# The RWKV-7 scan of a two-layer trunk: one product per head for scores and token-major keys, and loads in ten parts

## The chip, the cores and the metric

The kernel runs on one core of a Trainium2 chip. The metric is the device time of one execution in microseconds. The core has TensorE (PE in the rows; its loads of weights are listed apart as PEld), VectorE (DVE), ScalarE (ACT), GpSimd (POOL) and SyncE (SP). Each engine works through its own instructions in order and waits on semaphores for the others. Transfers are issued by SP, POOL and ACT and share 16 DMA engines.

## The reference

The trunk has two layers over 1024 latent and 256 context tokens of 1024 channels. The first mixes by pooling and attention, the second by a bidirectional RWKV-7 recurrence with 16 heads of 64 channels; each is followed by an MLP. The change touches the recurrence alone:

```python
def wkv_scan(s0, decay, k, v, kk, a, r, reverse):
    ...
    def step(S, inp):
        w_t, k_t, v_t, kk_t, kka_t = inp[:5]
        S = (S * w_t[:, :, None, :]
             - jnp.einsum('bhij,bhj->bhi', S, kk_t)[..., None] * kka_t[:, :, None, :]
             + v_t[..., None] * k_t[:, :, None, :])
        y = jnp.einsum('bhij,bhj->bhi', S, inp[5]) if emit else None
        return S, y
...
    for d, reverse in enumerate((False, True)):
        decay_c, k_dc, a_c = dirs_c[d]
        s_ctx, y_c = wkv_scan(s0, decay_c, k_dc, v_c, kk_c, a_c, r_c, reverse)
        decay, k_d, a = dirs[d]
        _, y_d = wkv_scan(s_ctx, decay, k_d, v, kk, a, r, reverse)
```

Both directions start on the context tokens, whose outputs aren't needed in this layer, and go on over the latent ones.

## The kernel before

The recurrence is computed in chunks of 64 tokens. Per chunk, direction and head it becomes products of 64x64 tiles: scores between tokens of the chunk, the inverse of a triangular matrix made from them, and products with the state that is carried from chunk to chunk. A stage ahead of the scan writes, per chunk and direction, four features per head to DRAM (`ft`). The scan loads them as FT, a tile of 128 partitions with eight pairs of heads: the even head of a pair lies on partitions 0 to 63, the odd one on 64 to 127 (`e` in the code), and the four features of 64 tokens stand behind each other. Features 2 and 3 of a head are the keys and their like, which serve as the 128 weight columns of a product; features 0 and 1 are the read side and the removal side.

The scan (`l1_scan`, from about 2213 to 2677 us) has 20 steps: 4 of context, then 16 of latent tokens. A step has two halves, one for each direction `d`. Each half works on the chain of chunk `s` (`chain_x`, `carry`, `chain_u`, `readout_state`, `chain_s`, `readout_values`) and, in between, on what chunk `n = s + 1` needs beforehand (`scores_k`, `token_major`, `stack`, `scores_r`; with `d` = 1 also `compose1` and `compose2`, which put together the inverse from blocks of 32). All of it is issued in the order in which it stands in the loop, under a manual schedule, so the order of each engine is that of the code. `fill()` puts a paced number of operations of a background generator between them: inverses of blocks on VectorE (L1511, L1515) up to about step 13, then parts of the readout.

Names on TensorE in a half step, in order: `xp` (chain_x, L1669), `sa` (scores_k, L1602), `tm` (token_major, four transposes of 128x128 for heads 0 to 3, L1632), `up` (chain_u, L1677), with `d` = 1 the first `p` (compose1, L1644), `tm` again, `yp` (readout_state, L1688), `sp` (chain_s, L1716), `yp` (readout_values, L1700), `sr` (scores_r, L1618), with `d` = 1 the second `p` (compose2, L1658). Context halves have no `yp` and no `sr`. A float32 matmul of the code stands as two instructions in the profile.

ScalarE copies results out of PSUM: `XS` from `xp`, `D<-up`, `TM` from `tm`, `yt` from `yp`, `p1s` and `TT` from `p`, and inside SBUF `D<-SS` (carry) and `Z<-FT` (stack). VectorE multiplies the scores by masks: `Z<-sa` (L1604), `Q<-sr` (L1622), and updates the state SS (L1722 and L1726). `sa`, `sr` and `tm` share a pool of four PSUM tiles of one bank each. GpSimd issues the load of FT, 1 MB, two steps ahead at the end of each half; SyncE issues the loads of the inverses' blocks (G, ZT, TT; eight transfers) at the end of a step, the values (`D<-v1scr`) and the stores of `yt`.

Of the kernel before, what the change touches and what calls it, by code (L numbers as in the profile page):

```python
# [58 lines left out]
class Trunk:  # L59
# [1466 lines left out]
    def l1_scan(self):  # L1526
        nc, a = self.nc, self.a
        with ExitStack() as es:
# [5 lines left out]
            scps = self.pool(es, "scps1", 4, PSUM)  # L1534
# [3 lines left out]
            FTs = [cp.tile([128, 8, 4, CH], F32, name=f"FT{i}") for i in range(4)]  # L1538
# [4 lines left out]
            st = (slice(0, 64), slice(64, 128))  # L1543

# [9 lines left out]
            W = {s: dict(lat=s >= NCC, F=[0, 0], Z=[0, 0], Q=[0, 0], TM=[0, 0], D=[0, 0], Y=[0, 0]) for s in range(NSTEP)}  # L1554
# [20 lines left out]
            def load_inverses(s):  # L1575
                w = W[s]
                TT = TTs[s % 2]
                ZT = zs.tile([128, 2, 8, 32], F32, tag="ZT", name="ZT")
                G = zs.tile([128, 2, 8, 32], F32, tag="G", name="G")
                q = lambda x, bl, e: x.rearrange("(s b c e) i t -> i s b e c t", s=2, b=2, e=2)[:, s % 2, bl, e]  # L1580
                dq = nc.sync
                for e in range(2):
# [6 lines left out]
                w["TT"], w["ZT"], w["G"] = TT, ZT, G  # L1589

            def stack(s, d):

                for e in range(2):
                    nc.scalar.copy(out=W[s]["Z"][d][0:64, :, e], in_=W[s]["F"][d][st[e], :, 1])

            def scores_k(s, d):
                F = W[s]["F"][d]
                Z = W[s]["Z"][d] = zp.tile([128, 8, 2, CH], F32, tag="Z", name="Z")
                sa = scps.tile([128, 8, CH], F32, tag="sc", name="sa")
                for h in range(8):  # L1600
                    for e in range(2):
                        nc.tensor.matmul(out=sa[st[e], h], lhsT=F[st[e], h, 3], rhs=F[st[e], h, 1], start=True, stop=True)  # L1602
                for e in range(2):
                    nc.vector.tensor_tensor(  # L1604
                        out=Z[64:128, :, e], in0=sa[st[e]], in1=masks[st[e], d, 2:3].to_broadcast([64, 8, CH]), op=ALU.mult
                    )

            def scores_r(s, d):

                w = W[s]  # L1610
                if not w["lat"]:
                    return
                F = w["F"][d]
                Q = w["Q"][d] = zp.tile([128, 8, 2, CH], F32, tag="Q", name="Q")
                sr = [scps.tile([128, 8, CH], F32, tag="sc", name="sr") for _ in range(2)]
                for h in range(8):
# [4 lines left out]
                for e in range(2):  # L1621
                    nc.vector.tensor_tensor(  # L1622
                        out=Q[:, :, e], in0=sr[e], in1=masks[:, d, 1:2].to_broadcast([128, 8, CH]), op=ALU.mult
                    )

            def token_major(s, d, h0):
                w = W[s]
                if h0 == 0:
                    w["TM"][d] = zp.tile([128, 8, 128], F32, tag="TM", name="TM")
                tm = scps.tile([128, 4, 128], F32, tag="sc", name="tm")  # L1630
                for j in range(4):
                    nc.tensor.transpose(  # L1632
                        out=tm[:, j], in_=w["F"][d][:, h0 + j, 2:4].rearrange("p a t -> p (a t)"), identity=self.ident
                    )
                nc.scalar.copy(out=w["TM"][d][:, h0:h0 + 4], in_=tm)

            def compose1(s):

                w = W[s]
                p1 = chps.tile([128, 2, 8, 32], F32, tag="ch", name="p1")  # L1640
# [6 lines left out]
                w["p1"] = zs.tile([128, 2, 8, 32], F32, tag="p1s", name="p1s", bufs=1)  # L1647
# [16 lines left out]
            def chain_x(s, d):  # L1664
                w = W[s]
                xp = chps.tile([128, 8, CH], F32, tag="ch", name="xp")
                for h in range(8):
                    for e in range(2):
                        nc.tensor.matmul(out=xp[st[e], h], lhsT=w["Z"][d][:, h, e], rhs=w["D"][d][:, h, e], start=True, stop=True)  # L1669
# [11 lines left out]
            def readout_state(s, d):  # L1681
# [4 lines left out]
                for h in range(8):  # L1686
                    for e in range(2):
                        nc.tensor.matmul(  # L1688
                            out=yp[st[e], h], lhsT=w["F"][d][st[e], h, 0], rhs=SS[d][st[e], h], start=h == 0, stop=True,
# [3 lines left out]
            def readout_values(s, d):  # L1693
# [4 lines left out]
                for h in range(8):  # L1698
                    for e in range(2):
                        nc.tensor.matmul(  # L1700
                            out=yp[st[e], h], lhsT=w["Q"][d][:, h, e], rhs=w["D"][d][:, h, e], start=False, stop=True, skip_group_check=True
# [7 lines left out]
            def chain_s(s, d):  # L1709
# [9 lines left out]
                t = hp_.tile([128, 8, CH], F32, tag="t", name="t", bufs=1)  # L1719
                src = sp  # L1720
                if s:
                    nc.vector.tensor_tensor(out=t, in0=sp, in1=SS[d], op=ALU.add)  # L1722
                    src = t
# [57 lines left out]
            for d in range(2):  # L1781
                scores_k(0, d)
                stack(0, d)
                for h0 in (0, 4):
                    token_major(0, d, h0)
# [9 lines left out]
            for s in range(NSTEP - 1):  # L1795
# [4 lines left out]
                for d in range(2):  # L1800
# [81 lines left out]
    def readout_weight(self, k):  # L1882

        if k not in self.rst:
            self.readout_weight_load(k)
        ip, zp = self.rwp
        pool, tag = {
            8: (ip, "M"), 0: (ip, "X"), 1: (zp, "TM"), 2: (ip, "BK"), 3: (zp, "Z"), 4: (zp, "Q"), 5: (zp, "TM"), 6: (zp, "Z"), 7: (zp, "Q"),
        }[k]
        w = [pool.tile([128, D], F32R, tag=tag, name=f"rwo{i}{k}") for i in "hl"]  # L1890
# [327 lines left out]
```

## Time and profile before

| | us |
|---|---|
| median of 3 runs | 3549.33 |
| range of the 3 runs | 3537.39 to 3551.44 |
| the profiled execution | 3559.48 |
| its span in the profile | 3557.6 |

The profile and its trace are of one execution, and its rows add up to its own span, which is 10 us longer than the median. Its mean granted clock of TensorE is 0.962 of full speed. Times in rows are microseconds from the start of the span, durations are microseconds unless a row says ns, and idle time of an engine that nobody waits for costs nothing.

### The profile page before, as it was taken

What the parts mean: (1) busy time and instruction counts of PE and PEld (TensorE: products, weight loads), DVE (VectorE), ACT (ScalarE), POOL (GpSimd) and SP (SyncE); (2) the same over time, 40 slices, a digit from 0 to 9 for tenths busy, and PEclk for the clock granted to TensorE, in tenths of its full rate; (3) what the DMA queues carried; (4) which work ended last, traced back from release to release, by engine and by line L of the source; (5) the groups of instructions that cost most, each with busy time, mean ns of one, the idle gap of its engine ahead of it and who ended that gap; (6) DMA issues with size and microseconds to landing.
All of it is one profiled execution on the core that took longest, in us unless ns stands there. A gap on an engine that the chain in (4) does not pass through costs nothing. (4 is left out here: it accounts for less than half of the span.)

```text
span 3557.6 us, 64666 instructions
## 1 busy us (share of the span) xinstructions
PE 3327.8 (94%) x26794; PEld 2790.3 (78%) x26794; DVE 2054.7 (58%) x3879; ACT 1432.3 (40%) x2667; POOL 342.3 (10%) x450
## 2 busy tenths in 40 slices
PE   8999889999999999989988876899988899999998
PEld 4787767888888888868878776788886788888887
DVE  4255555344444444596658996888775734444446
ACT  4244446312121211266767664655554521111112
POOL 0010110000000000024420001010031200000000
PEclk9999989999999999999989897899988999999999
DMA  8433344222222211143227678777773411111112
GB/s 274 151 92 87 97 131 130 89 83 83 83 84 83 74 46 36 42 148 99 71 69 221 210 233 241 170 185 201 200 204 104 164 50 48 48 48 48 48 48 77
DMA packets 426517, 409.24 MB, mean 115 GB/s; under 512 B 149664, under 2 KB 360480, under 8 KB 422128
## 3 DMA queue, kind: packets, MB, share of 16 engines
q1 hardware_dynamic: 405376, 321.55, 30.8%
q0 software_dynamic: 18624, 81.80, 6.8%
q8 instruction: 210, 3.44, 0.4%
q10 hardware_dynamic: 2224, 1.77, 0.2%
q14 instruction: 83, 0.68, 0.1%
HBM read 292.54 MB, written 112.49 MB: 114 GB/s over the span
## 5 line engine op out<-in xcount | busy, mean ns | idle before, releaser
L916 DVE TENSOR_TENSOR yacc<-yps,yacc 128x512 f32<-128x512 f32 x540 | 369.7, 690 | 305.2 <-PE yps L93 304.8
L74 ACT CAST wh<-st 128x1024 fp32r<-128x1024 f32 x160 | 165.0, 1049 | 759.8 <-PE yps L93 557.8
L93 PE MATMUL yps<-wh,xh 128*128 128x512 f32 x1152 | 453.8, 394 | 5.0 <-DVE yacc L916 3.4
L93 PE MATMUL yps<-wh,xl 128*128 128x512 f32 x1152 | 449.0, 390 | 0.7 <-DVE xl L75 0.7
L93 PE MATMUL yps<-wl,xh 128*128 128x512 f32 x1152 | 449.4, 390 | 0.0
L75 DVE TENSOR_TENSOR wl<-st,wh 128x1024 fp32r<-128x1024 f32 x160 | 194.2, 1228 | 277.4 <-ACT wh L74 277.2
L93 PE MATMUL acc<-h2h,wh 128*128 128x426 f32 (+3 forms) x768 | 275.1, 358 | 3.0 <-ACT y L671 3.0
L93 PEld LDWEIGHTS yps<-wh,xh 128*128 128x128 f32 x1152 | 216.4, 188 | 73.0 <-DVE yacc L916 14.0
L93 PE MATMUL acc<-h2h,wl 128*128 128x426 f32 (+3 forms) x768 | 273.6, 356 | 0.0
L93 PE MATMUL acc<-h2l,wh 128*128 128x426 f32 (+3 forms) x768 | 273.4, 356 | 0.0
L93 PEld LDWEIGHTS yps<-wh,xl 128*128 128x128 f32 x1152 | 216.5, 188 | 47.9 <-DVE xl L75 2.3
L93 PEld LDWEIGHTS yps<-wl,xh 128*128 128x128 f32 x1152 | 216.7, 188 | 44.9 <-issue 1.7
L898 DVE TENSOR_TENSOR r<-r 128x428 f32<-128x428 f32 (+4 forms) x164 | 102.4, 624 | 241.9 <-ACT r L897 241.9
L93 PE MATMUL acc<-mh,wh 128*128 128x256 f32 (+1 forms) x640 | 214.8, 337 | 4.3 <-ACT mh L74 4.2
L93 PE MATMUL acc<-ml,wh 128*128 128x256 f32 (+1 forms) x640 | 214.0, 334 | 0.0
L93 PE MATMUL acc<-mh,wl 128*128 128x256 f32 (+1 forms) x640 | 213.4, 334 | 0.0
L93 PE MATMUL acc<-h2bh,wh 128*128 128x512 f32 (+3 forms) x544 | 211.3, 388 | 1.4 <-ACT wh L74 0.7
L93 PE MATMUL acc<-h2bl,wh 128*128 128x512 f32 (+3 forms) x544 | 211.1, 388 | 1.0 <-DVE h2bl L288 1.0
L93 PE MATMUL acc<-h2bh,wl 128*128 128x512 f32 (+3 forms) x544 | 210.9, 388 | 0.3 <-DVE wl L75 0.3
L897 ACT ACTIVATE r<-acc 128x428 f32<-128x428 f32 (+4 forms) x164 | 89.1, 543 | 293.0 <-PE acc L93 267.9
L93 PEld LDWEIGHTS acc<-h2h,wh 128*128 128x128 f32 x768 | 144.6, 188 | 15.9 <-issue 5.1
L74 ACT CAST xh<-r 128x428 fp32r<-128x428 f32 (+4 forms) x164 | 93.2, 569 | 148.1 <-DVE r L898 148.1
(319 smaller groups left out, 7042.1 us busy)
## 6 DMA issues: line engine op xcount, KB each, us to landing
st<-in_mlp_w SPq DMA_DIRECT2D x128, 512.0 KB
ft<-F SPq DMA_DIRECT2D x64, 512.0 KB
FT<-ft POOLq DMA_DIRECT2D x32, 1024.0 KB, 7.1
adas<-in_ada_w POOLq DMA_DIRECT2D x112, 256.0 KB, 3.8
adas<-in_ada_w SPq DMA_DIRECT2D x80, 256.0 KB
x<-x SPq DMA_DIRECT2D x28, 512.0 KB
bias<-in_bias SPq DMA_DIRECT2D x64, 192.0 KB
ls<-ls SPq DMA_DIRECT2D x80, 128.0 KB
```

The costliest lines, as they stand in the source:

```text
L74: self.nc.scalar.copy(out=hi, in_=src)
L75: self.nc.vector.tensor_tensor(out=lo, in0=src, in1=hi.bitcast(F32), op=ALU.subtract)
L93: self.nc.tensor.matmul(out=ps, lhsT=lhs[x], rhs=rhs[y], start=first and i == 0, stop=last and i == 2)
L897: nc.scalar.activation(out=r, in_=ps, func=AF.Relu)
L898: nc.vector.tensor_tensor(out=r, in0=r, in1=r, op=ALU.mult)
L916: nc.vector.tensor_tensor(out=yacc[t][:, n], in0=ps, in1=yacc[t][:, n], op=ALU.add)
```

## The change

Three products become one. For two pairs of heads at a time (`g` = 0 to 3), `scores(s, d, g)` multiplies the 128 columns of features 2 and 3 with three blocks of 64 columns that stand side by side in FT: an identity, feature 0 and feature 1. The identity's block gives the transposed keys (what `tm` gave), the second `sr`, the third `sa`, together 192 columns per head and one PSUM tile of two banks per group; the pool has two of them in place of four tiles of one bank. In context halves the middle block is left out, in the last step the identity. FT gets a fifth block per pair of heads for the identity, which VectorE writes once, eight copies ahead of the scan. VectorE masks a group at a time into one tile ZQ (Z and Q before), four times a half, and ScalarE copies the transposed keys into TM, four times a half. The copies `Z<-FT` move into `carry()`. The temporary of the state's update is gone (SS is updated in place), and `p1s` lives in G.

The load of FT becomes four parts of two pairs each, and the load of the inverses two parts, one for each `e`. They are put on a list when a half ends its `readout_values`, and issued one by one at five places of a half (`loads()`).

```diff
-            scps = self.pool(es, "scps1", 4, PSUM)
+            scps = self.pool(es, "scps1", 2, PSUM)
...
-            FTs = [cp.tile([128, 8, 4, CH], F32, name=f"FT{i}") for i in range(4)]
+            FTs = [cp.tile([128, 8, 5, CH], F32, name=f"FT{i}") for i in range(4)]
...
+            for t in FTs:
+                for e in range(2):
+                    nc.vector.tensor_copy(out=t[st[e], :, 0], in_=self.ident[st[e], st[e]].unsqueeze(1).to_broadcast([64, 8, CH]))
...
-            def load(s, d):
+            def load(s, d, parts=range(4)):
...
-                (nc.scalar if s == 0 else nc.gpsimd).dma_start(out=F[:, :, f0:], in_=self.ft[s, d, :, :, f0:])
+                for i in parts:
+                    w["got"].add((d, i))
+                    hs = slice(2 * i, 2 * i + 2)
+                    (nc.scalar if s == 0 else nc.gpsimd).dma_start(out=F[:, hs, 1 + f0:], in_=self.ft[s, d, :, hs, f0:])
+
+            due = []
+
+            def loads():
+
+                if due:
+                    due.pop(0)()
...
+            def scores(s, d, g):
...
+                ps = scps.tile([128, 2, 512], F32, tag="sc", name="sc")
+                p4 = ps[:, :, 0:384].rearrange("p e (j f t) -> p j e f t", j=2, f=3)
+                f = slice(0, 3) if w["lat"] and more else slice(1, 3) if w["lat"] else slice(0, 3, 2)
+                for j in range(2):
                     for e in range(2):
                         nc.tensor.matmul(
-                            out=sr[e][:, h], lhsT=F[st[e], h, 2:4].rearrange("p a t -> p (a t)"), rhs=F[st[e], h, 0], start=True, stop=True
+                            out=p4[:, j, e, f], lhsT=F[st[e], 2 * g + j, 3:5].rearrange("p a t -> p (a t)"), rhs=F[st[e], 2 * g + j, f],
+                            start=True, stop=True,
                         )
...
+                if w["lat"]:
                     nc.vector.tensor_tensor(
...
+                        out=w["ZQ"][d][:, hs].rearrange("p j e f t -> p j e (f t)"),
+                        in0=ps[:, :, 0:384].rearrange("p e (j n) -> p j e n", j=2)[:, :, :, CH:],
+                        in1=masks[:, d, 1:3].rearrange("p f t -> p (f t)").unsqueeze(1).unsqueeze(1).to_broadcast([128, 2, 2, 2 * CH]),
+                        op=ALU.mult,
                     )
...
+                if more:
+                    nc.scalar.copy(out=w["TM"][d][:, hs].rearrange("p j (e i) -> p j e i", e=2), in_=p4[:, :, :, 0])
...
                     for e in range(2):
                         nc.scalar.copy(out=W[s]["D"][d][0:64, :, e], in_=SS[d][st[e]])
+                    stack(s, d)
...
                     chain_x(s, d)
                     carry()
-                    scores_k(n, d)
-                    if n + 1 < NSTEP:
-                        token_major(n, d, 0)
+                    for g in range(2):
+                        scores(n, d, g)
+                    loads()
                     fill()
                     chain_u(s, d)
                     if d:
                         compose1(n)
-                    if n + 1 < NSTEP:
-                        token_major(n, d, 4)
-                    stack(n, d)
+                    scores(n, d, 2)
+                    loads()
                     fill()
                     readout_state(s, d)
                     chain_s(s, d)
                     readout_values(s, d)
+                    if s + 2 < NSTEP:
+                        for i in range(4):
+                            due.append(partial(load, s + 2, d, (i,)))
+                            if d and i % 2:
+                                due.append(partial(load_inverses, s + 2, (i // 2,)))
+                    loads()
                     fill()
-                    scores_r(n, d)
+                    scores(n, d, 3)
                     if d:
                         compose2(n)
-                    if s + 2 < NSTEP:
-                        load(s + 2, d)
+                    loads()
+                    loads()
                     fill()
-                if s + 2 < NSTEP:
-                    load_inverses(s + 2)
```

How it moves instructions, first on TensorE, in a latent half step with `d` = 1. Before:

```order
L1669 MATMUL xp<-D,Z 64x64 x16
L1602 MATMUL sa<-FT_19565 64x64 x16
L1632 MATMUL tm<-ident,FT_19565 128x128 x4
L1677 MATMUL up<-XS_19567,TT_19568 64x64 x16
L1644 MATMUL p_23217<-ZT,G 32x32 x32
L1632 MATMUL tm<-ident,FT_19565 128x128 x4
L1688 MATMUL yp<-SS,FT_19563 64x64 x16
L1716 MATMUL sp<-D,TM 64x64 x16
L1700 MATMUL yp<-D,Q 64x64 x16
L1618 MATMUL sr<-FT_19565 128x64 x16
L1658 MATMUL p_23351<-TT_19569,p1s 32x32 x32
```

And with the change, where `sc` is the new product:

```order
L1681 MATMUL xp<-D,ZQ 64x64 x16
L1628 MATMUL sc<-FT_19565 128x192 x8
L1689 MATMUL up<-XS_19567,TT_19568 64x64 x16
L1656 MATMUL p_22962<-ZT,G 32x32 x32
L1628 MATMUL sc<-FT_19565 128x192 x4
L1700 MATMUL yp<-SS,FT_19563 64x64 x16
L1728 MATMUL sp<-D,TM 64x64 x16
L1712 MATMUL yp<-D,ZQ 64x64 x16
L1628 MATMUL sc<-FT_19565 128x192 x4
L1670 MATMUL p_23081<-TT_19569,G 32x32 x32
```

Four groups of 16, 4, 4 and 16 became groups of 8, 4 and 4; the rest kept its order. With `d` = 0 the two rows of `p` are missing. On ScalarE the same half step with `d` = 0 stood as follows before:

```order
L1670 COPY XS_19566<-xp 128x512 [waits PE_49]
L1736 COPY D<-SS 64x8x64 [waits DVE_49]
L1736 COPY D<-SS 64x8x64
L1635 COPY TM<-tm 128x512 [waits PE_49]
L1679 ACTIVATE D<-up 64x8x64 [waits PE_49,Activation_49]
L1679 ACTIVATE D<-up 64x8x64 [waits Activation_49]
L1635 COPY TM<-tm 128x512 [waits PE_49]
L1594 COPY Z<-FT_19562 64x8x64 [waits DMASW6_49]
L1594 COPY Z<-FT_19562 64x8x64
L1704 COPY yt<-yp 128x512 [waits DMAHW6_49,DMAHW5_49,PE_49]
```

And with the change, with the semaphores that each waits for in brackets (DVE is VectorE's, DMASW the loads of GpSimd):

```order
L1682 COPY XS_19566<-xp 128x512 [waits PE_49]
L1747 COPY D<-SS 64x8x64 x2
L1610 COPY ZQ<-FT_19565 64x8x64 [waits DMASW2_49,DMASW3_49,DMASW1_49,DMASW0_49]
L1610 COPY ZQ<-FT_19565 64x8x64
L1646 COPY TM<-sc 128x256 [waits DVE_49] x2
L1691 ACTIVATE D<-up 64x8x64 [waits PE_49,Activation_49]
L1691 ACTIVATE D<-up 64x8x64 [waits Activation_49]
L1646 COPY TM<-sc 128x256 [waits DVE_49]
L1716 COPY yt<-yp 128x512 [waits DMAHW7_49,DMAHW0_49,PE_49]
L1646 COPY TM<-sc 128x256 [waits DVE_49]
```

The copies of FT moved from behind `D<-up` to ahead of it, two copies `TM` stand ahead of it where one did, and `TM` waits for VectorE where it waited for TensorE. On SyncE the transfers of a step stood as follows before, those of the inverses together at its end:

```order
L1584 DMA G<-ls 32x16x32
L1585 DMA ZT<-ltt_23392 32x16x32
L1588 DMA TT_19568<-lt_23391 32x16x32 x2
L1584 DMA G<-ls 32x16x32
L1585 DMA ZT<-ltt_23392 32x16x32
L1588 DMA TT_19568<-lt_23391 32x16x32 x2
L1570 DMA D<-v1scr 64x1024
L1707 DMA yscr<-yt 64x512 x2
```

And with the change:

```order
L1601 DMA G<-ls 32x16x32
L1602 DMA ZT<-ltt_22454 32x16x32
L1605 DMA TT_19569<-lt_22453 32x16x32 x2
L1583 DMA D<-v1scr 64x1024
L1719 DMA yscr<-yt 64x512 x2
L1601 DMA G<-ls 32x16x32
L1602 DMA ZT<-ltt_22454 32x16x32
L1605 DMA TT_19569<-lt_22453 32x16x32 x2
```

The second half of the inverses moved behind the values and the stores of the following half step.

## Rows read from the trace of the kernel before

**Rows 1.** The page, section 1: busy us, share of the span, instructions.

```profile
PE 3327.8 (94%) x26794; PEld 2790.3 (78%) x26794; DVE 2054.7 (58%) x3879; ACT 1432.3 (40%) x2667; POOL 342.3 (10%) x450
```

**Rows 2.** Busy us by stretch of PE, PEld, DVE, ACT, POOL; clock, DMA share, GB/s.

```profile
2213.00:2288.70 75.70, 64.77 (x1666) 57.60 (x1666) 57.42 (x136) 50.43 (x86) 7.61 (x12) 0.91 0.81 174
2288.70:2538.20 249.50, 228.81 (x5926) 209.98 (x5922) 216.65 (x521) 141.57 (x240) 23.67 (x41) 0.93 0.68 183
2538.20:2667.80 129.60, 114.88 (x2947) 105.59 (x2944) 84.06 (x100) 77.31 (x129) 35.75 (x23) 0.92 0.76 218
```

**Rows 3.** Timeline of TensorE, 2477 to 2490: start, us, engine, line, operation.

```profile
2477.51 1.15 PE L1669 MATMUL xp<-D,Z 128*64 128x64 f32 x32
2478.59 1.15 PE L1602 MATMUL sa<-FT 64*64 64x64 f32 x32
2479.67 0.66 PE L1632 MATMUL tm<-ident,FT 128*128 128x128 f32 x4
2480.26 1.15 PE L1677 MATMUL up<-XS,TT 64*64 64x64 f32 x32
...
2486.14 2.00 PE L1618 MATMUL sr<-FT 64*128 64x64 f32 x32
2488.08 1.20 PE L1658 MATMUL p<-TT,p1s 32*32 32x32 f32 x64
2489.21 1.15 PE L1669 MATMUL xp<-D,Z 128*64 128x64 f32 x32
```

**Rows 4.** Waits of TensorE, 2213 to 2668: us in total, times, longest.

```profile
PE p L1644 <- issue: 10.1, 6, 4.1
...
PE sp L1716 <- ACT D L1679: 2.5, 10, 0.5
...
PE tm L1632 <- issue: 0.3, 1, 0.3
```

**Rows 5.** Busy us by stretch, 2441.3 to 2448.1, columns as rows 2.

```profile
2441.30:2448.10 6.80, 5.97 (x83) 5.29 (x84) 5.38 (x13) 2.40 (x4) 0.00 (x0) 0.50 0.65 98
```

**Rows 6.** Timeline of all engines, 2459 to 2471; the idle time before in brackets.

```profile
2460.99 0.53 POOL L1566 DMA_DIRECT2D FT<-ft  x1 [0.72 <-ACT TM L1635]
...
2469.98 0.33 PE L1602 MATMUL sa<-FT 64*64 64x64 f32 x3 [2.36 <-issue]
```

**Rows 7.** DMA queues (packets, MB, share) and issues (KB, us to landing), 2213 to 2680.

```profile
q8 instruction: 85, 1.39, 1.3%
...
FT<-ft POOLq DMA_DIRECT2D x32, 1024.0 KB, 7.1
```

**Rows 8.** Timeline of TensorE in the attention, 160 to 162.2.

```profile
160.22 0.70 PE L731 MATMUL sc<-kT,qT 64*128 64x256 f32 x4 [0.61 <-ACT kT L338]
160.76 0.81 PE L736 MATMUL sl<-kT,qT 64*128 64x384 f32 x4
161.50 0.50 PE L93 MATMUL acc<-h1h,wh 128*128 128x512 f32 x1
```

**Rows 9.** Groups by line, 2289 to 2668: count, busy us, mean ns, idle before.

```profile
L1604 DVE TENSOR_TENSOR Z<-sa,masks 64x512 f32<-64x512 f32 x60 | 41.4, 690 | 17.2 <-PE sa L1602 16.1
L1622 DVE TENSOR_TENSOR Q<-sr,masks 128x512 f32<-128x512 f32 x62 | 39.7, 682 | 9.3 <-PE sr L1618 9.2
L1594 ACT COPY Z<-FT 64x512 f32<-64x512 f32 x60 | 37.1, 618 | 0.9
L1679 ACT ACTIVATE D<-up 64x512 f32<-64x512 f32 x60 | 35.5, 591 | 15.2 <-PE up L1677 14.3
L1635 ACT COPY TM<-tm 128x512 f32<-128x512 f32 x56 | 32.5, 581 | 7.7 <-PE tm L1632 6.9
...
L1518 DVE COPY M<-X 128x1024 f32<-128x1024 f32 x7 | 7.4, 1062 | 0.2
```

**Rows 10.** The chain that ended last, 2164 to 2240: start, us, what.

```profile
2177.66 10.23 DMA ls<-ls
```

**Rows 11.** Timeline of VectorE, 2602 to 2614.

```profile
2606.46 2.77 DVE L1955 TENSOR_TENSOR y<-y,var 128x1024 f32<-128x1024 f32 x1
```

More of the change, by code (lines that the diff above doesn't have):

```diff
@@ L1552, in rows_of @@
                 return t[c * CH:(c + 1) * CH]
-            W = {s: dict(lat=s >= NCC, F=[0, 0], Z=[0, 0], Q=[0, 0], TM=[0, 0], D=[0, 0], Y=[0, 0]) for s in range(NSTEP)}
+            W = {s: dict(got=set(), lat=s >= NCC, F=[0, 0], ZQ=[0, 0], TM=[0, 0], D=[0, 0], Y=[0, 0]) for s in range(NSTEP)}
             lt_, ltt_ = self.lt_, self.ltt_
@@ L1608, in scores_r @@
-            def scores_r(s, d):
+                    nc.scalar.copy(out=W[s]["ZQ"][d][0:64, :, e, 1], in_=W[s]["F"][d][st[e], :, 2])
+            def scores(s, d, g):
                 w = W[s]
-                if not w["lat"]:
-                    return
                 F = w["F"][d]
-                Q = w["Q"][d] = zp.tile([128, 8, 2, CH], F32, tag="Q", name="Q")
-                sr = [scps.tile([128, 8, CH], F32, tag="sc", name="sr") for _ in range(2)]
-                for h in range(8):
+                more = s + 1 < NSTEP
+                if g == 0:
+                    w["ZQ"][d] = zp.tile([128, 8, 2, 2, CH], F32, tag="ZQ", name="ZQ")
+                    if more:
+                        w["TM"][d] = zp.tile([128, 8, 128], F32, tag="TM", name="TM")
+                assert (d, g) in w["got"]
+                ps = scps.tile([128, 2, 512], F32, tag="sc", name="sc")
+                p4 = ps[:, :, 0:384].rearrange("p e (j f t) -> p j e f t", j=2, f=3)
+                f = slice(0, 3) if w["lat"] and more else slice(1, 3) if w["lat"] else slice(0, 3, 2)
+                for j in range(2):
@@ L1622, in scores_r @@
+                hs = slice(2 * g, 2 * g + 2)
+                if w["lat"]:
                     nc.vector.tensor_tensor(
-                        out=Q[:, :, e], in0=sr[e], in1=masks[:, d, 1:2].to_broadcast([128, 8, CH]), op=ALU.mult
-                    )
[L1626 to L1633, printed above, removed]
-                    )
-                nc.scalar.copy(out=w["TM"][d][:, h0:h0 + 4], in_=tm)
+                        out=w["ZQ"][d][:, hs].rearrange("p j e f t -> p j e (f t)"),
+                        in0=ps[:, :, 0:384].rearrange("p e (j n) -> p j e n", j=2)[:, :, :, CH:],
+                        in1=masks[:, d, 1:3].rearrange("p f t -> p (f t)").unsqueeze(1).unsqueeze(1).to_broadcast([128, 2, 2, 2 * CH]),
+                        op=ALU.mult,
+                    )
+                else:
+                    nc.vector.tensor_tensor(
+                        out=w["ZQ"][d][64:128, hs, :, 1], in0=p4[64:128, :, :, 2],
+                        in1=masks[64:128, d, 2:3].unsqueeze(1).to_broadcast([64, 2, 2, CH]), op=ALU.mult,
+                    )
@@ L1646, in compose1 @@
                             )
-                w["p1"] = zs.tile([128, 2, 8, 32], F32, tag="p1s", name="p1s", bufs=1)
+                w["p1"] = w["G"]
                 for e in range(2):
@@ L1668, in chain_x @@
                     for e in range(2):
-                        nc.tensor.matmul(out=xp[st[e], h], lhsT=w["Z"][d][:, h, e], rhs=w["D"][d][:, h, e], start=True, stop=True)
+                        nc.tensor.matmul(out=xp[st[e], h], lhsT=w["ZQ"][d][:, h, e, 1], rhs=w["D"][d][:, h, e], start=True, stop=True)
                 nc.scalar.copy(out=XSs[d], in_=xp)
@@ L1688, in readout_state @@
                         nc.tensor.matmul(
-                            out=yp[st[e], h], lhsT=w["F"][d][st[e], h, 0], rhs=SS[d][st[e], h], start=h == 0, stop=True,
+                            out=yp[st[e], h], lhsT=w["F"][d][st[e], h, 1], rhs=SS[d][st[e], h], start=h == 0, stop=True,
                             skip_group_check=True,
@@ L1700, in readout_values @@
                         nc.tensor.matmul(
-                            out=yp[st[e], h], lhsT=w["Q"][d][:, h, e], rhs=w["D"][d][:, h, e], start=False, stop=True, skip_group_check=True
+                            out=yp[st[e], h], lhsT=w["ZQ"][d][:, h, e, 0], rhs=w["D"][d][:, h, e], start=False, stop=True, skip_group_check=True
                         )
@@ L1781, in l1_scan @@
             for d in range(2):
-                scores_k(0, d)
+                for g in range(4):
+                    scores(0, d, g)
                 stack(0, d)
-                for h0 in (0, 4):
-                    token_major(0, d, h0)
                 load(1, d)
@@ L1886, in readout_weight @@
         ip, zp = self.rwp
[L1887 to L1890, printed above, removed]
+        if k in (3, 4, 6, 7):
+            w = zp.tile([128, 2, D], F32R, tag="ZQ", name=f"rwo{k}")
+            w = [w[:, i] for i in range(2)]
+        else:
+            pool, tag = {8: (ip, "M"), 0: (ip, "X"), 1: (zp, "TM"), 2: (ip, "BK"), 5: (zp, "TM")}[k]
+            w = [pool.tile([128, D], F32R, tag=tag, name=f"rwo{i}{k}") for i in "hl"]
         self.split(w[0], w[1], self.rst.pop(k))
```

33 lines of the change are left out of this document (12 added, 21 removed).

## The prediction

> **What bounds the kernel now.** I read the page first, for the share of each engine: TensorE is busy for 94% of the span [rows 1], so the kernel as a whole follows TensorE. That is an average over stages, and the change touches one of them, the scan, so next I cut the scan by the steps' first `xp` into three stretches [rows 2]: context steps 0 to 3 (75.7 us, 18.9 a step), latent steps 4 to 13 with background inverses on VectorE (249.5 us, 24.95 a step), and latent steps 14 to 18 without them (129.6 us, 25.9 a step). The reader is to see two things there. TensorE idles in every stretch, although it has the most work, and its mean granted clock is 0.91 to 0.93, not 1. And VectorE is busy for 216.65 of 249.5 us (87%) in the second stretch, but for 84.06 of 129.6 (65%) in the third, which nevertheless has the longest steps. So the third is bound by TensorE, and the second by both, closely.
>
> How long would a step take if TensorE never waited? The timeline of a half step at full clock [rows 3] gives it by start to next start: the half with d=1 runs from 2477.51 to 2489.21, 11.70 us. The half with d=0 lacks the two groups of `p` (1.13 each, 2488.08 to 2489.21), so it is 9.44, and a step 21.14. Against 25.9 in the third stretch 4.8 us a step are lost. The waits of TensorE [rows 4] say where: ten of their rows name "issue", from 10.1 us before `p` down to 0.3 before `tm`, 34.0 us in all over 19 steps, that is 1.8 a step; the row on the longest engine wait of the chain, `sp` on ACT's `D`, has only 2.5. The rest is the clock: after such a hole the stretch 2441.3 to 2448.1 runs at a granted clock of 0.50, the lower of the two levels (1.2 of 2.4 GHz) [rows 5]. Stretch by stretch the lost clock is 0.09 x 75.7 + 0.07 x 249.5 + 0.08 x 129.6 = 34.7 us [rows 2]. Holes and clock together are some 69 us of 455.
>
> What is late in a hole? At 2467.61 TensorE stops, and `sa` resumes at 2469.98 after 2.36 us of "issue". The load of FT had been issued 6.6 us before, at 2460.99 [rows 6]; such a load is 1 MB and takes 7.1 us to land, and the instructions come over a DMA queue of their own, 85 packets of 16 KB (1.39 MB) in the scan [rows 7]. I read the hole as an instruction packet late behind the burst of loads. The trace shows that they coincide; it does not prove the cause.
>
> **The change part by part.** *Products on TensorE.* A latent half loses `sa` 1.08 us, two `tm` of 0.59 and `sr` 1.94 [rows 3], 4.20 in all. It gains eight pairs of 64x128 products with 192 columns. No such pair exists before. The nearest are attention's: four rows (a pair) take 0.54 us at 256 columns and 0.74 at 384 [rows 8], 0.2 per 128 columns; `sr`'s pair at 64 columns takes 1.94/8 = 0.24, and 0.24 + 0.2 gives 0.44 at 192, as the line through the two attention rows does. Bounds: 0.405, if time is in proportion to columns (0.54 x 192/256), and 0.54. So eight cost 3.5 (3.2 to 4.3), and a half saves 0.7 (-0.1 to 1.0). In the context half a pair has 128 columns, some 0.34, eight 2.7 against 2.26 for `sa` and `tm`: 0.4 lost, over seven such halves 3.
>
> *The new order on ACT.* In a d=0 half ACT now runs `XS` (0.58), two `D<-SS` and two `ZQ<-FT` (0.62 each), `TM0`, `TM1` (half of 0.58 each, bounds 0.29 and 0.58), then two `D<-up` (0.59) [rows 9]. With `XS` at 1.3 us after the half's start, `TM0` ends near 4.7 and `D` near 6.25. On TensorE `xp`, two groups `sc` and `up` end at 1.08 + 1.75 + 1.08 = 3.9. The third `sc` needs `TM0` gone from its PSUM buffer, so it waits 0.8 us; then `sc` 0.88 and `yp` 1.08 end at 6.7, after `D`, and `sp` does not wait. In the d=1 half `p` (1.13) stands before the third `sc` and covers the wait. A step is thus 21.14 - 1.4 + 0.8 = 20.6 (20.0 to 22.1) in place of 21.14. What is queued behind `TM` on ACT is `D<-up`, which `sp` needs, and `yt`.
>
> *VectorE.* Four evictions of 128x512 replace two of Z (0.69) and two of Q (0.68) [rows 9]: nothing. Background work and its pace are as before. So the second stretch keeps its VectorE work, 21.7 us a step. Its idle 3.3 holds the gaps between 521 instructions and waits; I take half for gaps, so the floor is 23.3 (21.7 to 24.95). When the third `sc` is late VectorE waits too, about 1.0 a step, by the same 0.8 and its half of the next. That makes 24.3.
>
> *The loads.* Same bytes, in four parts of 256 KB and two halves of the inverses, spread over a step; SP and POOL issue more instructions, but POOL was busy for 23.67 of 249.5 us [rows 2]. TensorE also fetches fewer instructions: 16 products in place of 40 in a half. I take it that 60% of the holes and of the slow clock after them go, between none and all: a guess, halfway and a little more, as the cause is only seen to coincide. The Trainium skill, Runtime: NRT & Kernel Launch, section Instruction fetch mechanics, says that crossing a block of instructions is mostly hidden; the holes of 2.36 us don't agree with that here, though no row proves them fetches. By that page the holes are something else and this term is zero, the first rival.
>
> A new wait can come with it: the second half of the inverses goes out behind the `yscr` stores of the next step, so `p` may wait. Bounds 0 and 1 us a step; in the sum I let the 0.4 that remains of the holes stand for it.
>
> *Before the scan.* Eight copies of the identity, 64x512 each, on VectorE: half a copy of 128x1024 (1.06) each [rows 9], 4.2 us, while VectorE makes the last features. Behind them the path is one of transfers, `ls` 10.23 us [rows 10], that start when these features are done, so I count half, 2 us (0 to 4.2).
>
> *Sum.* Third stretch: 25.9 to 20.6 + 0.4 x 4.8 = 22.5, so -3.4 a step, over five -17. Second: 24.95 to 24.3, over ten -6.5. First: +3 for the products, about -3 for fewer holes, 0. Before: +2. Together -21.5. The profiled execution took 3559.48, 10 us above the median of the runs shown, 3549.33; on its base the sum is 3538.0, on the median's 3527.8.
>
> **The rivals.** A, *the holes stay*. If the holes don't come from the load's burst, or the same bytes do it in parts as well, the third stretch gains 0.5 a step (2.7), the second nothing, the prelude loses 2, and the time is 3549. For it speaks that the bytes and queues are the same; against it, the 1 MB load just ahead of the hole that is read above. The Trainium skill, DMA: Bandwidth & Descriptors, section Queues, rings and completion order, says that a DMA engine takes turns between queues by packets; by that the length of a load matters little to another queue's packet, which speaks for A, too.
>
> B, *slower: VectorE holds ACT and ACT holds TensorE*. `TM` now waits for VectorE's product of the same group. Before, it waited for TensorE alone. `TM0` and `TM1` are covered while VectorE ends the second eviction within about 1.9 us of TensorE's second group; beyond that each microsecond delays `D<-up`, `sp` and the state. In the third stretch VectorE has readout operations of up to 2.77 us [rows 11], in the second it is 87% busy. With 2 us a step over 15 steps (+30), 2 for the prelude, and 12 back from the holes, the time is 3569. Against it: VectorE's evictions stand in the same place of its order as before.
>
> C, *more: holes and clock are cured*. Then the third stretch runs at 20.6 (-26.5) and the second at VectorE's 23.3 (-16.5), +2 before: 3508. For it speaks that the lost time is there to take; against it, that other transfers share the engines: the share of the DMA engines is 0.68 to 0.81 [rows 2].
>
> **How the numbers follow.** Chances: forecast 0.46, A 0.20, B 0.16, C 0.18. Half a per cent, 17.7 us, is about what a measurement of this kernel can tell from no change. Faster than 3531.6: two thirds of the forecast's cases (its own terms vary by some 10 us), and all of C: 0.48. Slower than 3567: most of B and a little of A: 0.15. The rest, 0.37, is within. The range 3503 to 3562 takes in the forecast, A, most of C and the mild half of B. The likeliest case's own range is 3518 to 3542.
>
> **What would show it.** Right: the rows of "issue" on TensorE fall from 34 to about 14 us, the clock of steps 14 to 18 rises to 0.97, these steps take 22.5 us, eight `sc` pairs take 3.5 us, and the third `sc` waits for ACT in the d=0 half. Wrong by A: the holes keep their sum. Wrong by B: `sp` or `sc` wait for ACT, and ACT's `TM` for VectorE, by over 1 us a half. The largest single doubt is the 60%.

## The result: slower by 0.94%

With the change the kernel takes 3578.98 us (median of 4 runs, 3577.45 to 3580.91), before it 3550.39 (4 runs); the ratio is 1.0094, 95% interval 1.0075 to 1.0113. The forecast was 3528, faster, with a range of 3503 to 3562.

The stretches of the scan, cut by the steps' first `xp`, show where it went, here for one execution of the kernel after, with the columns of [rows 2].

```profile
2210.20:2295.20 85.00, 68.36 (x1537) 59.20 (x1536) 64.05 (x162) 49.71 (x99) 20.73 (x29) 0.89 0.75 159
2295.20:2557.30 262.10, 218.41 (x5126) 190.59 (x5120) 206.28 (x508) 141.94 (x280) 69.99 (x101) 0.91 0.69 172
2557.30:2690.30 133.00, 107.07 (x2570) 94.44 (x2562) 76.46 (x98) 77.90 (x146) 55.06 (x49) 0.91 0.76 207
```

Against [rows 2] the context steps grew from 75.7 to 85.0 us, steps 4 to 13 from 249.5 to 262.1, steps 14 to 18 from 129.6 to 133.0. TensorE's own work shrank in the second and third: 228.81 to 218.41 and 114.88 to 107.07 us busy. So it waits more. These are its waits from 2210 to 2690 (total us, times, longest), to be read beside [rows 4]:

```profile
PE sc L1628 <- ACT TM L1646: 41.3, 34, 2.9
PE p L1656 <- DMA ZT<-ltt: 24.7, 11, 5.1
PE up L1689 <- ACT XS L1682: 7.1, 12, 0.9
PE p L1670 <- issue: 2.8, 1, 2.8
...
PE yp L1712 <- issue: 1.4, 1, 1.4
...
PE yp L1700 <- issue: 0.5, 1, 0.5
```

The rows of issue fell from 34.0 to 4.7 us, further than forecast. In their place stand 41.3 us in which the new product `sc` waits for the copies `TM`, and 24.7 us in which `p` waits for the inverses.

**The wait for TM, with d=1.** The next three fences are timelines of the kernel after around 2410 (start, duration, engine, line): TensorE, then VectorE, then ACT.

```profile
2407.07 0.92 PE L1628 MATMUL sc<-FT 64*128 64x192 f32 x8
...
2409.00 0.92 PE L1628 MATMUL sc<-FT 64*128 64x192 f32 x8
2412.50 1.64 PE L1628 MATMUL sc<-FT 64*128 64x192 f32 x8 [2.58 <-ACT TM L1646]
2414.07 1.97 PE L1689 MATMUL up<-XS,TT 64*64 64x64 f32 x32
...
2421.05 0.92 PE L1628 MATMUL sc<-FT 64*128 64x192 f32 x8
2421.90 1.20 PE L1670 MATMUL p<-TT,G 32*32 32x32 f32 x64
```

```profile
2407.50 0.68 DVE L1733 TENSOR_TENSOR SS<-sp,SS 128x512 f32<-128x512 f32 x1
2408.22 0.69 DVE L1737 TENSOR_TENSOR SS<-SS,pcs 128x512 f32<-128x512 f32 x1
...
2411.36 0.68 DVE L1634 TENSOR_TENSOR ZQ<-sc,masks 128x512 f32<-128x512 f32 x1
```

```profile
2412.08 0.37 ACT L1646 COPY TM<-sc 128x256 f32<-128x256 f32 x1 [4.31 <-DVE ZQ L1634]
```

The fourth `sc` of a half ends at about 2408. VectorE masks it at 2411.36, behind the state's update and six background operations. Only then does ACT copy TM, at 2412.08, and only that frees one of the two PSUM buffers for the second `sc` of the next half, which has waited 2.58 us. The rest of the half runs late, and from 2412.5 to 2416 at a granted clock of 0.51 (`up` 1.97 us against 1.15). The last two rows give the price of the product: 2421.05 to 2421.90 for two pairs, 0.425 a pair, where 0.44 was forecast.

**The wait for TM, with d=0.** VectorE's mask of the fourth group, then ACT, then TensorE, where a half of the kernel after begins:

```profile
2450.02 0.68 DVE L1634 TENSOR_TENSOR ZQ<-sc,masks 128x512 f32<-128x512 f32 x1
```

```profile
2450.73 0.37 ACT L1646 COPY TM<-sc 128x256 f32<-128x256 f32 x1 [2.31 <-DVE ZQ L1634]
2451.00 1.16 ACT L1674 COPY TT<-p 32x512 f32<-32x512 f32 x2
2452.19 0.58 ACT L1682 COPY XS<-xp 128x512 f32<-128x512 f32 x1
2452.80 1.26 ACT L1747 COPY D<-SS 64x512 f32<-64x512 f32 x2
2454.08 1.25 ACT L1610 COPY ZQ<-FT 64x512 f32<-64x512 f32 x2
2455.23 0.63 ACT L1646 COPY TM<-sc 128x256 f32<-128x256 f32 x2
```

```profile
2449.70 1.15 PE L1681 MATMUL xp<-D,ZQ 128*64 128x64 f32 x32
...
2452.82 1.15 PE L1689 MATMUL up<-XS,TT 64*64 64x64 f32 x32 [0.47 <-ACT XS L1682]
2455.64 0.92 PE L1628 MATMUL sc<-FT 64*128 64x192 f32 x8 [1.67 <-ACT TM L1646]
```

This is the wait of the third `sc` that was forecast at 0.8 us; it is 1.67, after 0.47 in which `up` waits for `XS`. `XS` begins 2.49 us after `xp`; the forecast had 1.3, which is what the kernel before shows, with the copies TT in the same place ahead of it:

```profile
2465.45 1.15 PE L1669 MATMUL xp<-D,Z 128*64 128x64 f32 x32
2465.57 1.16 ACT L1662 COPY TT<-p 32x512 f32<-32x512 f32 x2 [2.48 <-PE p L1658]
2466.75 0.59 ACT L1670 COPY XS<-xp 128x512 f32<-128x512 f32 x1
```

With the change TT begins 1.2 us later, behind the fourth TM, which has waited for the mask. So the late mask of the fourth group has a share in both waits for TM. Of their 41.3 us the third group has 24.7, the second 16.6.

**The wait for the inverses.** SyncE and TensorE in step 14 of the kernel after:

```profile
2564.66 4.25 SPq L1583 DMA_DIRECT2D D<-v1scr  x1
2569.01 1.18 SPq L1719 DMA_DIRECT2D yscr<-yt  x2
2570.24 1.51 SPq L1601 DMA_DIRECT2D G<-ls  x1
2571.79 0.55 SPq L1602 DMA_DIRECT2D ZT<-ltt  x1
```

```profile
2571.49 0.24 PE L1656 MATMUL p<-ZT,G 32*32 32x32 f32 x2
2576.82 1.91 PE L1656 MATMUL p<-ZT,G 32*32 32x32 f32 x62 [5.08 <-DMA ZT<-ltt]
```

The second half of the inverses is issued when `p` is already there: SyncE spent 4.25 us on the values and then waited its turn with the stores. ZT goes out at 2571.79 and `p` resumes 5.03 us later.

### The profile page after: what moved, and what is told of

It is laid out like the page before. It is cut to its first block, busy times and chain, and to the rows that moved or that the text cites. A ratio compares the mean times of both kernels' runs of the same rounds, so it can differ in the third digit from the quotient of the medians.

```text
span 3575.9 us, 62535 instructions
## 1 busy us (share of the span) xinstructions
PE 3312.1 (93%) x25466; PEld 2760.9 (77%) x25466; DVE 2049.2 (57%) x3903; ACT 1434.6 (40%) x2743; POOL 428.7 (12%) x564
## 3 DMA queue, kind: packets, MB, share of 16 engines
q1 hardware_dynamic: 405376, 321.55, 30.4%
q10 hardware_dynamic: 2320, 1.77, 0.2%
## 5 line engine op out<-in xcount | busy, mean ns | idle before, releaser
L1628 PE MATMUL sc<-FT 64*128 64x192 f32 (+1 forms) x1280 | 149.1, 362 | 47.9 <-ACT TM L1646 42.1
```

The costliest lines, as they stand in the source:

```text
L1628: nc.tensor.matmul(out=p4[:, j, e, f], lhsT=F[st[e], 2 * g + j, 3:5].rearrange("p a t -> p (a t)"), rhs=F[st[e], 2 * g + j, f], start=True ...
```

## The experiments

Twelve kernels and three single profiles followed. From the steps' first `xp` in the timeline of each kernel (s0, s4, s14, s19) the table has the lengths between, the time of the last, and the sums of TensorE's rows of issue and of the two waits from s0 to s19, in us (a dash where there is none over 2 us); each is one execution. The last column is the measured ratio to the kernel before, with its interval.

| kernel | steps 0-3 | 4-13 | 14-18 | s19 at | issue | sc for TM | p for ZT | ratio |
|---|---|---|---|---|---|---|---|---|
| before | 75.9 | 249.5 | 129.6 | 2667.8 | 34.0 | - | 2.7 | 1 |
| before, second profile | 75.2 | 241.8 | 121.3 | 2649.3 | 30.4 | - | - | - |
| the change | 85.1 | 262.1 | 132.9 | 2690.3 | 4.7 | 41.3 | 24.7 | 1.0094 (1.0075-1.0113) |
| parts alone | 81.0 | 268.8 | 129.3 | 2681.7 | 22.1 | - | 31.2 | 1.0066 (1.0047-1.0084) |
| product alone | 88.7 | 247.4 | 130.4 | 2679.9 | 14.0 | 42.4 | 2.5 | 1.0044 (1.0029-1.0059) |
| FT in parts alone | 84.2 | 241.3 | 130.7 | 2664.2 | 36.6 | - | 3.6 | 1.0002 (0.9988-1.0016) |
| inverses first, products of before | 77.3 | 262.0 | 135.1 | 2680.1 | 26.0 | - | 2.9 | 1.0082 (1.0058-1.0106) |
| the change, fourth group ahead | 83.4 | 263.1 | 134.6 | 2689.6 | 3.7 | 23.0 | 46.1 | 1.0092 (1.0077-1.0107) |
| the change, inverses first | 83.8 | 244.9 | 128.4 | 2669.5 | 13.6 | 44.8 | 4.9 | 1.0026 (1.0015-1.0037) |
| and copies later | 79.6 | 236.5 | 133.7 | 2658.6 | 10.8 | 26.6 | 10.4 | 1.0009 (0.9997-1.0020) |
| and TM ahead of the mask | 83.1 | 241.6 | 132.0 | 2664.8 | 18.1 | - | 8.3 | 1.0022 (1.0009-1.0036) |
| copies later, inverses at the step's end | 81.2 | 237.0 | 132.7 | 2654.9 | 20.5 | 22.9 | 5.7 | 0.9986 (0.9974-0.9997) |
| the same, FT whole | 83.1 | 237.1 | 126.8 | 2656.0 | 21.2 | 25.9 | 2.4 | 0.9998 (0.9983-1.0014) |
| the same as the last but one, product split | 82.9 | 258.0 | 129.8 | 2682.5 | 18.9 | 13.9 | 3.2 | 1.0071 (1.0051-1.0091) |
| the same, not split, fourth group ahead | 80.8 | 225.9 | 127.2 | 2641.4 | 14.1 | 24.0 | 6.8 | 0.9970 (0.9958-0.9982) |

The two profiles of before differ by 8 us in each of the latent stretches, so a difference of that size between two rows says nothing; the ratios decide.

**One part of the change at a time.** The parts of the loads under the products of before (the edit is that of `load`, `load_inverses` and `loads` in the diff, nothing else):

> The kernel before, with only the loads changed: FT in four parts and the inverses in two, issued one by one at the same places as in the change; products, PSUM pool and copies as before. Theory: the holes of TensorE came from the burst of the 1 MB load, so the parts alone cure them: rows of issue on TensorE fall from 34 us to under 8, while the late second half of the inverses makes p wait 20 to 25 us as in the changed kernel. Net 0 to -20 us against before: 3530 to 3550. Rival 1, the holes went because TensorE has fewer instructions: then they stay at 25 to 34 us and with p's waits the time is 3570 or more. Rival 2, the ten parts cost time by themselves and are the whole loss: 3575 or more, with few holes.

3571.3 us, 24 more than before, and 22.1 us of issue. Two of its waits:

```profile
PE p L1655 <- DMA ZT<-ltt: 31.2, 11, 6.5
PE sa L1613 <- DMA FT<-ft: 6.1, 4, 2.6
```

The wait of `p` was longer than the 20 to 25 us expected, and the cure of the holes did not come: at most a third went. The time is the first rival's (3570 or more), with issue a little under its 25. The other part alone keeps the new products and takes the loads of before:

> The changed kernel with the loads of before (1 MB at a half's end, all inverses at a step's end). Theory: sc waits for the copies TM about as in the changed kernel (some 40 us), p's waits for the inverses fall under 5 us, and most of the holes come back (15 to 30 us of issue): 3570 to 3600, that is, the product alone is slower than before. Rival 1 (fewer instructions cure the holes): issue stays under 8 us, and with p's waits gone the time is 3545 to 3560. Rival 2 (the parts are the whole loss): 3530 to 3550, faster than before.

3565.7 us, 18 more than before: the product alone is slower too, though less than the theory's 3570 to 3600. `sc` waits 42.4 us as forecast, and issue is 14.0, just under the theory's range. So both parts lose. The two losses (24 and 18) add up to more than the 28.6 of both together; that they overlap, since both stop TensorE in the same steps, is a reading and not shown.

**Which part of the loads.** Only the order of the list is changed, the inverses ahead of FT's parts:

```diff
                     if s + 2 < NSTEP:
+                        for i in range(2 * d):
+                            due.append(partial(load_inverses, s + 2, (i,)))
                         for i in range(4):
                             due.append(partial(load, s + 2, d, (i,)))
-                            if d and i % 2:
-                                due.append(partial(load_inverses, s + 2, (i // 2,)))
```

> The changed kernel with one change of order: both halves of the inverses are put on the list ahead of the parts of FT of the half step with d=1, so that neither goes out behind the stores of the next step. Theory: p's wait for the inverses falls from 25 us to under 5 and part of the slow clock behind it with it: 3540 to 3560. Rival (p's wait only uncovers the next late thing, the wait of sc for TM): p's wait goes, that of sc grows by the same, 3570 to 3580.

3557.6 us, 21 less than the change, and `p` waits 4.9 in place of 24.7; `sc`'s waits stay at 44.8. The late inverses cost the change some 21 us; the theory holds. The same order under the products of before was to repair the parts there:

> The products of before, FT in four parts and the inverses in two, with both halves of the inverses ahead of the parts of FT of the half with d=1. Theory: of the loss of 24 us that the parts alone made, p's wait for the inverses (31 us) is the cause, and it goes; with fewer holes than the 34 us of before the time is 3530 to 3545, below before. Rival (smaller parts cost by themselves, through more issues or a later landing): p's wait goes but the time stays above 3555.

```profile
PE sa L1613 <- DMA FT<-ft: 26.9, 16, 6.9
...
PE p L1655 <- DMA ZT<-ltt: 2.9, 1, 2.9
```

3570.5 us: `p` no longer waits, but `sa` does, 26.9 us, for FT, whose four parts for the half with d=1 now go out one or two places later. `sa` wants all of FT at the start of a half, where `sc` wants one part per group. The theory's time was wrong and the rival's (above 3555) came, but not for its reason: the wait moved. That left FT's parts by themselves, the inverses at the step's end as before:

> The products of before and the inverses loaded at a step's end as before; FT alone in four parts along the step. Theory: the late p was the cost of the parts, so without it the time is 3530 to 3548, with rows of issue on TensorE of 10 to 25 us. Rival (the parts of FT themselves cost): 3555 or more.

3547.8 us, the same as before (ratio 1.0002), at the theory's upper end, but not for its reason: issue is 36.6 us, more than the 34.0 of before and above the 10 to 25 expected. Smaller loads of the same bytes neither cost time nor cure the holes.

**What holds TM.** First VectorE's order in the changed kernel, the fourth group's products ahead of background work:

```diff
+                    scores(n, d, 3)
                     loads()
                     fill()
-                    scores(n, d, 3)
```

> The changed kernel with the fourth group of sc written ahead of the third piece of background work, so that VectorE masks it before and not after some four to six background operations; TensorE's order stays. Theory: the second group's wait of the next half, for the copy TM of this fourth group, falls from 20 us (14 long ones of up to 2.9) to under 6, the third group's wait of 25 us (1.67 in most halves with d=0) stays, p's wait stays or grows a little: 3555 to 3572. Rival (VectorE is late in any order, since it is the bound): the wait moves to the third group or to the state's update, 3575 to 3582.

3582.5 us. `sc`'s waits fell from 41.3 to 23.0: the second group's from 17 to 3, the third's, which were to stay at 25, to 20. So the place of the fourth mask held the second group. `XS` is on time again, 1.31 us after `xp`, and in halves with d=0 the third `sc` then most often waits 1.04:

```profile
2347.47 1.15 PE L1681 MATMUL xp<-D,ZQ 128*64 128x64 f32 x32
...
2348.78 0.59 ACT L1682 COPY XS<-xp 128x512 f32<-128x512 f32 x1
...
2352.24 0.92 PE L1628 MATMUL sc<-FT 64*128 64x192 f32 x8 [1.04 <-ACT TM L1646]
```

But `p` now waits 46.1 us for the inverses: TensorE arrives sooner at a transfer that is no sooner there. The forecast of `sc`'s waits held, that of `p`'s did not, and the time is near the rival's upper end. Then ACT's order, with the inverses first:

```diff
-                    stack(s, d)
+                    pile.append((s, d))
...
                     scores(n, d, 2)
+                    stacks()
                     loads()
```

Here `stacks()` makes the copies `ZQ<-FT` that `carry()` made ahead of TM.

> The kernel with the inverses first, and in addition the copies of FT into ZQ taken from their place behind the copies of the state and put behind the third copy TM, so that ACT makes TM and D<-up 1.24 us earlier in each half. Theory: they stand on the chain of the context steps (which took 84 us against 76 before) and in front of the TM for which the third sc waits 1.67 us in halves with d=0; the context steps fall to 78 to 80 and sc's waits for TM from 45 to 25 us: 3538 to 3550. Rival (TM is late because VectorE is late, not ACT): waits and context steps stay, 3554 to 3562.

3547.2 us, 10 less than without the edit; `sc`'s waits 26.6 and the context steps 79.6 us: as expected. It is the third group's waits that went, from 27 to 4 us; the second's, from 18, are 23. Then the order of the two readers of a group's PSUM tile:

> As the one with the copies later, and the copy TM of a group is written ahead of its mask product, so that ACT waits for TensorE alone and VectorE for ACT. Theory (ACT's wait for VectorE is what holds D<-up and the buffers): sc's wait for TM falls under 10 us, 5 to 12 us less than the one with the copies later. Rival (the order of the two only turns the wait round: VectorE, which has the most work in the steps with inverses, now waits for ACT): the same time or up to 10 us more, with VectorE's products waiting for ACT in place of ACT for VectorE.

3550.9 us, 4 more, which is not clear of noise, and the wait has turned round, with VectorE waiting for ACT and `sc` for VectorE:

```profile
DVE ZQ L1636 <- ACT TM L1634: 52.2, 33, 6.9
...
PE sc L1628 <- DVE ZQ L1636: 33.6, 28, 5.1
...
PE sc L1628 <- DVE ZQ L1643: 6.6, 6, 2.3
```

That is the rival. Turning the order of the two readers gained nothing; the buffer is held for both either way.

**The loads once more, under the new product,** with the copies later. Inverses at the step's end, then FT whole as well:

> The kernel with the copies later, FT in parts along the step, and the inverses together at a step's end as before. Theory: of the loads only the place of the inverses matters; p's wait (10 us with the inverses first) falls under 5, sc's wait for FT (one of 4.7) goes, since nothing delays its parts, sc's waits for TM stay near 27: 3538 to 3546. Rival (the inverses at the end bring the holes back, as a burst): issue 25 to 35 us and 3548 to 3560.

> As the one with the inverses at the end, but FT loaded whole at a half's end, as before. With the one before it this prices the parts of FT alone, under the new product. If the burst of 1 MB makes holes: issue 10 to 20 us more than with parts, 5 to 20 us slower. If it does not (as FT's parts alone, under the products of before, left 36.6 us of issue against 34.0): the two agree within 5 us and 5 us of issue.

3539.3 and 3547.5 us; issue 20.5 and 21.2. The first is as expected in time and faster than before by 0.14%; `p`'s wait is 5.7 us, just above the 5 named, and its issue lies under the rival's 25 to 35. Parts and whole loads have the same issue, so here too parts don't cure the holes. The 8 us between the two are more than the 5 named, but their intervals overlap (0.9974-0.9997, 0.9983-1.0014), so whether parts gain time under this product is not settled. Next, do the holes follow the number of TensorE's instructions? Each product of 192 columns is split into one of 64 and one of 128:

> As the one with the inverses at the end, but each product of 192 columns as two of 64 and 128, in latent halves: the same result and the same waits to meet, 32 products in place of 16 and 64 more instructions and loads of weights for TensorE in a half. Theory now (holes follow the number of TensorE's instructions between waits): issue rises to 20 to 35 us from about 11. Rival (holes only hide behind other waits): sc's waits get smaller by the longer products and issue rises by no more than that, to 10 to 16 us. The products take about (0.24 + 0.34) x 8 in place of 0.42 x 8 a half, 1.3 us, 2.5 us a step where TensorE is the bound: 15 to 30 us slower than without the split in either case.

3570.2 us, 31 more than without the split, and issue 18.9, not more than 20.5. The theory on the count of instructions falls. The rival's 10 to 16 did not come either: both ranges started from 11, and the kernel without the split has 20.5.

**What makes the holes.** Three profiles, each of one execution (a second run of before beside them took 3542.8 us), bear on the step on which the forecast's 60% stood. The first is of the kernel before once more; the second leaves out FT's loads from step 6 on, the third those of the inverses:

> The kernel before, unchanged: a second profile of it, to see how much the sum of TensorE's rows of issue varies from one execution to the next. Every theory: 28 to 40 us, steps 4 to 13 in 245 to 254 us.

> The kernel before, with FT not loaded from step 6 on: these steps compute with the features that lie in the buffers, so the output is left wrong, at the same work for each engine. Theory of the prediction (the burst of the 1 MB load makes the holes): issue falls from 34 to under 12 us, most of what is left before step 4. Rival (other transfers or no transfer make them): issue stays at 25 us or more.

> The kernel before, with the inverses' blocks (G, ZT, TT, eight transfers a step in short pieces) not loaded from step 6 on: these steps compute with older blocks, so the output is left wrong, at the same work for each engine. If their short pieces hold up the instruction packets: issue falls from 34 to under 15 us. If the FT load does, or neither: it stays at 22 us or more.

3539.2, 3518.2 and 3533.4 us. The second profile of before has 30.4 us of issue, as expected, but its steps 4 to 13 are shorter than the 245 to 254 named. From 2320 us on, the rows of issue of the kernel without FT's loads sum to 5.7 us, all that there are:

```profile
PE yp L1701 <- issue: 2.4, 2, 1.6
PE sr L1619 <- issue: 1.6, 2, 1.0
PE tm L1633 <- issue: 0.9, 1, 0.9
PE up L1678 <- issue: 0.6, 1, 0.6
PE sp L1717 <- issue: 0.2, 1, 0.2
```

Over its whole scan they are 14.1, above the 12 expected, as 8.4 stand ahead of 2320. Before, seven rows of the stretch from 2320 in its second profile have 22.1 us, the first of them this:

```profile
PE yp L1700 <- issue: 5.8, 3, 2.5
```

Without the inverses' loads eight rows still sum to 20.1 us. So most holes go with FT's loads, as the prediction read it. What the loads cost is 21 to 25 us against the two single runs of before; the fastest of all runs of before, 3535.5, is still 17 us slower. The number of packets on all queues does not decide: from 2320 to 2640 the trace has 92 thousand with 65.9 MB before, 33 thousand with 60.8 MB without the inverses, where the holes stay, and 84 thousand with 41.9 MB without FT, where they go. The same bytes of FT in parts leave the holes where they are. Whether it is an instruction packet that comes late, as the prediction read it, no run shows.

**A version that beats both.** The three repairs together (copies later, inverses at the step's end, fourth group ahead of background work):

> As the one with the inverses at the end, with the fourth group ahead of the third piece of background work. In the changed kernel this took 18 us of sc's waits for TM and gave them to p, which waited for the late inverses; here these are not late. Theory: sc's waits for TM fall from 27 to under 12 us and the time with them: 3528 to 3540, faster than before by 0.2 to 0.5%. Rival (VectorE's total work sets the pace of steps 4 to 13): waits fall but the time stays within 4 us of the one without it.

3537.75 us, 0.9970 of before (0.9958 to 0.9982) and 41 us less than the change; the time is as forecast. `sc`'s waits stay at 24.0, so the fall from 27 to under 12 was wrong: the second group's went from 18 to 4 us, the third's grew from 5 to 20. Against the kernel without this edit (0.9986, interval 0.9974 to 0.9997) the gain is not clear of noise, and the 1.6 us between them are within the 4 that the rival named. Its stretches, in an execution 7 us under its median, columns as [rows 2]:

```profile
2207.50:2288.30 80.80, 67.79 (x1539) 58.97 (x1537) 63.34 (x159) 51.13 (x99) 21.06 (x30) 0.90 0.83 171
2288.30:2514.20 225.90, 202.74 (x5124) 178.33 (x5120) 206.79 (x511) 146.11 (x281) 69.92 (x99) 0.98 0.80 199
2514.20:2641.40 127.20, 107.43 (x2566) 94.79 (x2560) 78.82 (x98) 78.64 (x146) 55.69 (x49) 0.91 0.78 211
```

Steps 4 to 13 take 22.6 us each, of which VectorE is busy for 20.7; the forecast's floor of 23.3 for them was too high. The context steps still take 5 us more than before.

## Why the prediction was wrong

By stretches, the sum had -17 us for steps 14 to 18, -6.5 for steps 4 to 13, 0 for the context steps and +2 ahead of the scan. The profiles of before and after show +3.4, +12.6, +9.3 and -2.6.

- **Right: the price of the product.** 0.425 us a pair against 0.44. TensorE's busy time fell with it.
- **Right in sign, wrong in reason: the holes.** Issue was to fall from 34 to 14 and fell to 4.7. The holes go with FT's loads, shown by leaving these out; that parts of a load cure them is refuted (36.6 with FT's parts alone; 20.5 and 21.2 with and without parts under the new product). Why they fell so far under the change stays open. One reading is that the other waits hide them, and then they give no time back. It fits most of the table (the two kernels with the longest waits for TM and ZT together, 66 and 69 us, have the fewest, 4.7 and 3.7), but the split kernel has less of these waits than the one without the split and no more issue. So it is argued, not shown.
- **The step that failed first: the wait of `p`.** The prediction named it with 0 to 1 us a step and put nothing in the sum beside the rest of the holes. It is 24.7 us, up to 5.1 at once, some 2.4 a step in steps 14 to 18, and taking it away gave 21 us back.
- **The second: ACT's order.** The term was a third `sc` late by 0.8 us in halves with d=0, 20.6 a step; the row shows 1.67, and `up` late by 0.47. ACT's order by itself was nearly priced right: with `XS` on time the wait is most often 1.04. The sum lacked that `XS` comes late, by the third point. Moving the copies `ZQ<-FT` behind TM gave 10 us.
- **The third: two buffers.** Rival B had TM behind VectorE and `sp` late by it. The place was another: the mask of the fourth group, behind background work, held the second group of the next half, and ACT's queue with it. `sp` waited for ACT's D only 2.5 us, as before. The argument against rival B, that VectorE's order is as before, was the error: the order is, but a buffer now hangs on it. Writing that group earlier took 18 us off these waits in the changed kernel.
- **The context steps** were put at nothing and lost 9 us. In the change 10.4 us of `sc`'s waits for TM, nine of them, stand there. With the copies later they lost 4 to 8 us. But FT in parts alone, under the products of before, takes 84.2 us for them as well, so the cause of the remainder stays open.
- **The clock** was to rise to 0.97 in steps 14 to 18 and stayed at 0.91: the new stops are followed by half clock like the holes, as at 2576 behind the longest wait of `p`:

```profile
2576.40:2583.20 6.80, 6.38 (x122) 5.76 (x124) 1.46 (x2) 2.50 (x4) 1.73 (x3) 0.50 0.20 49
```

## What to carry to other kernels

Before a product is merged, follow its PSUM buffers to their last reader: when two engines read a buffer in turn, whatever stands ahead of the first on its queue holds the next product of the third. When loads are spread, the one with the nearest reader goes first and not behind stores on the same queue, which cost 21 us here; the same list repaired one kernel and broke the other, as their products wanted the parts at different times. And a wait that is cured counts only once the next wait in its place has been priced.

## What was not expected of the hardware

One issue of the values (256 KB) kept SyncE's queue for 4.25 us at 2564.66 and 1.93 us at 2396.74, where the median of 38 such issues is 0.70; at 2564.66 the short transfers behind it were late by as much, and ZT took 5.03 us more to land. FT's loads cost 21 to 25 us in single runs, though no row of TensorE's waits in the scan before names them, and cutting them in four left the rows of issue where they were.
